# Four of eleven pairs of the first SwiGLU products by seven products of quarters

## The chip, the cores and the metric

The kernel runs on one core of a Trainium2 chip. The metric is the device time of one execution in microseconds (us); it is the median of three runs unless a profiled execution is named. Engines are named as in the profile: PE is TensorE (matmuls) and PEld its weight loads, DVE is VectorE, ACT is ScalarE, POOL is GpSimd, SP is SyncE, which issues most of the loads.

## The reference

Two layers over 512 tokens of width 1024. Each layer is a SwiGLU half step, a token mixer and a second SwiGLU half step, each followed by a layer norm. Four SwiGLUs in all, of hidden width 2816:

```python
def swiglu(x, w13, w2):
    a, b = jnp.split(x @ w13, 2, axis=-1)
    return (jax.nn.silu(a) * b) @ w2

for l in range(DEPTH):
    x = layer_norm(ALPHA * x + 0.5 * swiglu(x, ffn1_w13[l], ffn1_w2[l]), ln_g[l, 0], ln_b[l, 0])
    m = mixer(x, w_in[l], ...)
    x = layer_norm(ALPHA * x + m, ln_g[l, 1], ln_b[l, 1])
    x = layer_norm(ALPHA * x + 0.5 * swiglu(x, ffn2_w13[l], ffn2_w2[l]), ln_g[l, 2], ln_b[l, 2])
```

The change is in `x @ w13`, the first product of a SwiGLU. The mixer is not touched.

## The kernel before

**Arithmetic.** Every float32 operand of a large product is split into a high part (ScalarE copies it to fp32r, line 118) and a low part (VectorE subtracts the high part, line 119). A product is three matmuls: high by high, high by low, low by high. That is `split`, called by `weights` (line 121), which first loads a raw 128 x 1024 block of weights from HBM (line 124, on SP).

**First products.** The hidden width is 22 blocks of 128 features. For block j, `pa` gets the a columns and `pb` the b columns; each is 8 steps of the contraction by 3 matmuls with all 512 tokens as the moving operand (`proj`, line 143). `glu` (line 457) takes silu of `pa` on ScalarE (line 461) and multiplies it with `pb` on VectorE (line 462) into a room `r` of pair k, where k is j modulo 11: block k and block k + 11 make a pair. The pairs go in the order 8, 9, 10, 0 to 7. The first two blocks of a SwiGLU (except the very first) are done by halves of the tokens, 256 columns at a time, because the second half of x comes later.

**Second products.** `Seven` multiplies the activations with w2 by seven products of quarters in place of eight (Strassen's scheme in Winograd's form). It needs sums of quarters on both sides. `activation_sums(k)` (lines 291 to 318) makes those of pair k's activations. `weight_sums(k)` (lines 277 to 289) loads four quarters of w2 into two buffers `ra_w` and `rb_w` (lines 281 and 282, on SP), adds four times on VectorE (lines 283 and 288, three of them in place) and stores each sum to DRAM from POOL's queue (lines 284 and 289). `run` reads the sums back in its own order and does the products. Before the change both sums of pair k come right behind the second block of the pair, so one weight sum goes with every two blocks.

**Buffers.** Tiles of a tag share a fixed number of buffers:

| tag | buffers | what is in it |
|---|---|---|
| raw | 4 | raw weight blocks |
| w | 10 | high and low parts of weights, so five blocks |
| rs | 2 | `ra_w` and `rb_w` of a weight sum; squares of the norm; the changed kernel's rc and rd |
| sa | 3 | silu results, `t1` of a weight sum, `s12` of an activation sum |
| h ("slot") | 33 | x in parts (8), rooms, activation sums, early weights |
| ps | 8 | PSUM banks |

**Order.** The program is written as a straight list. A planner puts each engine's instructions in an order of its own from their dependences and their place in the list, and sets the waits; each engine then runs its list strictly in that order. `flow.tick` only hands out side tasks (transposes of x, the mixer's heads) between matmuls.

The functions that the diff touches:

Of the kernel before, what the change touches and what calls it, by code (L numbers as in the profile page):

```python
# [36 lines left out]
NF = DFF // P  # L40
# [42 lines left out]
def trunk(ctx: ExitStack, tc, x_in, xt_in, w13, w2, w_in, w_br, w_out, ln_g, ln_b, lb_in, hgn, sgg, sgb, sgws,  # L83
          sgbs, masks, tril_in, ident_in, out):
    nc = tc.nc
    V, S, G, PE = nc.vector, nc.scalar, nc.gpsimd, nc.tensor
# [3 lines left out]
    wk = ctx.enter_context(tc.tile_pool(name="wk", bufs=1))  # L90
    psum = ctx.enter_context(tc.tile_pool(name="psum", bufs=8, space=bass.MemoryType.PSUM))

    flow = Flow()
    MM = 216.0

    def bank(name):
        return psum.tile([P, 512], F32, tag="ps", name=name)
# [4 lines left out]
    def slot(name, dtype=F32):  # L102
        return big.tile([P, 2, 512], dtype, tag="h", name=name, bufs=NS)
# [10 lines left out]
    xh, xl = [None] * 4, [None] * 4  # L114


    def split(hi, lo, src):
        S.activation(hi, src, AF.Copy)  # L118
        V.tensor_tensor(lo, src, hi.bitcast(F32), op=ALU.subtract)  # L119

    def weights(src, name, early=False):

        raw = wk.tile([P, D], F32, tag="raw", name=f"r_{name}", bufs=NRAW)
        nc.sync.dma_start(raw, src)
        if early:
            hi, lo = (slot(f"{c}_{name}", F32R).rearrange("p a t -> p (a t)") for c in "hl")
        else:
            hi, lo = (wk.tile([P, D], F32R, tag="w", name=f"{c}_{name}", bufs=NW) for c in "hl")
        split(hi, lo, raw)
        return hi, lo  # L130

    NW = 10
    NS, NRAW, NSA = 33, 4, 3

    def proj(ps, w, c0, mov, nk=KT, n0=0, n=T):

        hi, lo = w
        i = 0
        for k in range(nk):
            cs = slice(c0 + k * P, c0 + (k + 1) * P)  # L140
            mh, ml = mov(k)
            for a, m in ((hi, mh), (hi, ml), (lo, mh)):
                PE.matmul(ps[:, n0:n0 + n], a[:, cs], m[:, n0:n0 + n], start=(i == 0), stop=(i == 3 * nk - 1))  # L143
                i += 1
            flow.tick(3 * MM * n / T)
# [5 lines left out]
    def begin_features():  # L151
        for q in range(4):
            xh[q], xl[q] = slot(f"xh{q}", F32R), slot(f"xl{q}", F32R)
# [26 lines left out]
    H = slice(0, 512), slice(512, 1024)  # L180
# [72 lines left out]
    def quads(name, dtype=F32):  # L253
        return slot(name, dtype).rearrange("p a t -> p (a t)").rearrange("p (q t) -> p q t", q=4)

    NH2 = NF // 2

    class Seven:
# [11 lines left out]

        def part(self, k, a):

            if k not in self.r:
                self.r[k] = quads(f"r{k}")
            return self.r[k][:, a::2, :]

        def weight_sums(self, k):
            w = self.w_of(k)
# [51 lines left out]
        def run(self, c, ln, last):  # L330
# [103 lines left out]
            for tt in range(2):  # L434
# [5 lines left out]
                add_to(xs[t], 0, c, F[tt], sums[t])  # L440
                norm(t, xs[t], sums[t], g, b, last)

    def ffn(l, i, last=False, first_of_all=False):
        made = list(range(Seven.KEPT, NH2)) + list(range(Seven.KEPT))
        seven = Seven(lambda k: w2[l, i, k])
        js = [j for k in made for j in (k, k + NH2)]

        def blocks(j, early=False):
            return (weights(w13[l, i, j], f"a{j}", early), weights(w13[l, i, NF + j], f"b{j}", early),
                    bank(f"pa{j}"), bank(f"pb{j}"))  # L450

        def pair_of(j, args, n0, n):
            wa, wb, pa, pb = args
            proj(pa, wa, 0, from_x, KT, n0, n)
            proj(pb, wb, 0, from_x, KT, n0, n)

        def glu(j, args):
            wa, wb, pa, pb = args
            k, a = j % NH2, j // NH2
            sa = wk.tile([P, T], F32, tag="sa", name="sa", bufs=NSA)  # L460
            S.activation(sa, pa, AF.Silu)
            V.tensor_tensor(seven.part(k, a), sa.rearrange("p (h t) -> p h t", h=2),  # L462
                            pb.rearrange("p (h t) -> p h t", h=2), op=ALU.mult)
            if a:
                seven.activation_sums(k)
                seven.weight_sums(k)

        start = 0 if first_of_all else 2
        first = [blocks(j, True) for j in js[:start]]
        need(0, 1)  # L470
        for z, j in enumerate(js[:start]):
            pair_of(j, first[z], 0, 256)
        need(2, 3)
        for z, j in enumerate(js[:start]):
            pair_of(j, first[z], 256, 256)
            glu(j, first[z])
        for z, j in enumerate(js[start:]):
            if z == 0 and first_of_all:
                begin_features()
                wa = load_wx(w13[l, i, j])  # L480
                for q in range(1, 4):
                    load_xt(q)
                wb = weights(w13[l, i, NF + j], "b0")
                args = wa, wb, bank("pa0"), bank("pb0")
            else:
                args = blocks(j)
            pair_of(j, args, 0, T)
            glu(j, args)
        seven.run(0.5 / ALPHA, (l, 2 * i), last)

    def gates():
# [353 lines left out]
    def load_xt(q):  # L845

        raw = wk.tile([P, D], F32, tag="raw", name=f"xt{q}", bufs=NRAW)
        nc.sync.dma_start(raw, xt_in[q])
        for k in range(2):
            split(xh[q][:, k, :], xl[q][:, k, :], raw[:, k * T:(k + 1) * T])  # L850

    def load_wx(w):

        raw = wk.tile([P, D], F32, tag="raw", name="r_a0", bufs=NRAW)
        hi, lo = (wk.tile([P, D], F32R, tag="w", name=f"{c}_a0", bufs=NW) for c in "hl")
        rx = wk.tile([P, D], F32, tag="raw", name="xt0", bufs=NRAW)
        for z in range(2):
            zs = slice(z * 512, (z + 1) * 512)
            nc.sync.dma_start(raw[:, zs], w[:, zs])
            nc.sync.dma_start(rx[:, zs], xt_in[0, :, zs])  # L860
            split(hi[:, zs], lo[:, zs], raw[:, zs])
            split(xh[0][:, z, :], xl[0][:, z, :], rx[:, zs])
        return hi, lo

    prep = flow.add(prepare(), 30000.0)
    for l in range(DEPTH):
        ffn(l, 0, first_of_all=(l == 0))
        if l == 0:
            flow.finish(prep)
        mixer(l, lb, om)  # L870
        ffn(l, 1, last=(l == DEPTH - 1))
# [98 lines left out]
```

## Time and profile before

| | |
|---|---|
| three runs | 2114.56, 2115.26, 2116.20 us; median 2115.26 |
| profiled execution | 2116.28 us, span 2114.5 us, granted TensorE clock 0.999 |
| busy: PE, DVE, ACT, POOL | 99%, 58%, 36%, 10% of the span |
| DMA | 381 MB, mean 180 GB/s |
| first products of the last SwiGLU | 1758 to 2000 us of the span |
| second product of the last SwiGLU | 2000 to 2098 us |

A line of the profile's groups reads: line, engine, operation, output<-inputs with buffer numbers left out, shape, how often, then busy us and mean ns of one, then the engine's idle time before such instructions and what ended it. A line of the timeline reads: start, length, engine, line, operation, tiles, shape, and in brackets the idle time before it with its releaser. The ends of matmuls are modelled, so spacing is read from starts or from the chain of work that ended last, whose pieces are start, length and what. The DMA lines give count, size and median us from issue to landing.

### The profile page before, as it was taken

How to read it: one execution, taken by the hardware profiler on the slowest of the kernel's cores; microseconds unless marked ns; L12 is line 12 of the kernel's file. 1: busy time of each engine (PE TensorE's matmuls, PEld its weight loads, DVE VectorE, ACT ScalarE, POOL GpSimd, SP SyncE). 2: the span in 40 equal slices, each digit the busy share in tenths (PEclk: the TensorE clock that was granted, in tenths of full speed). 3: DMA queues.
4: the chain of work that ended last, by engine and by line, in shares of the span. 5: the costliest groups of instructions: out<-in, count | busy, mean ns of one | idle time of the engine just before them, and what ended most of it. 6: DMA issues, size and time to landing. Idle time of an engine off the chain costs nothing. (4 is left out here: it accounts for less than half of the span.)

```text
span 2114.5 us, 26531 instructions
## 1 busy us (share of the span) xinstructions
PE 2096.8 (99%) x10024; PEld 1760.8 (83%) x10024; DVE 1226.2 (58%) x2019; ACT 771.4 (36%) x1090; POOL 211.4 (10%) x360
## 2 busy tenths in 40 slices
PE   8999999999999999999999999999999999999998
PEld 6888888888888988888898888888888889888886
DVE  5545578853535745548754456779444456454586
ACT  4222354223422422225522224552343224222363
POOL 0101102001000211101111010020010001110101
PEclk9999999999999999999999999999999999999999
DMA  7665777122242465567756566761222425555674
GB/s 267 216 211 177 247 262 256 44 77 89 81 156 93 176 235 177 195 210 268 248 192 233 178 208 234 270 230 41 90 81 91 143 95 208 205 200 198 223 258 146
DMA packets 113904, 381.01 MB, mean 180 GB/s; under 512 B 14320, under 2 KB 14576, under 8 KB 113776
## 3 DMA queue, kind: packets, MB, share of 16 engines
q1 hardware_dynamic: 88848, 291.68, 42.1%
q0 software_dynamic: 24928, 87.64, 10.9%
q8 instruction: 78, 1.28, 0.3%
q14 instruction: 50, 0.41, 0.1%
HBM read 311.11 MB, written 68.16 MB: 179 GB/s over the span
## 5 line engine op out<-in xcount | busy, mean ns | idle before, releaser
L143 PE MATMUL pa<-xh,h_a 128*128 128x512 f32 (+1 forms) x752 | 284.4, 378 | 6.2 <-ACT xh L118 6.1
L143 PE MATMUL pa<-xl,h_a 128*128 128x512 f32 (+1 forms) x752 | 284.5, 378 | 0.0
L143 PE MATMUL pa<-xh,l_a 128*128 128x512 f32 (+1 forms) x752 | 283.6, 377 | 0.0
L143 PE MATMUL pb<-xh,h_b 128*128 128x512 f32 (+1 forms) x752 | 282.8, 376 | 0.0
L143 PE MATMUL pb<-xh,l_b 128*128 128x512 f32 (+1 forms) x752 | 282.4, 375 | 0.0
L143 PE MATMUL pb<-xl,h_b 128*128 128x512 f32 (+1 forms) x752 | 282.3, 375 | 0.0
L119 DVE TENSOR_TENSOR l_b<-r_b,h_b 128x1024 fp32r<-128x1024 f32 x132 | 161.6, 1225 | 166.8 <-ACT h_b L118 166.3
L118 ACT ACTIVATE h_b<-r_b 128x1024 fp32r<-128x1024 f32 x132 | 140.0, 1061 | 303.6 <-PE pa L143 245.8
L462 DVE TENSOR_TENSOR r<-sa,pb 128x512 f32<-128x512 f32 x88 | 60.6, 688 | 302.0 <-PE pb L143 302.0
L118 ACT ACTIVATE h_a<-r_a 128x1024 fp32r<-128x1024 f32 (+1 forms) x89 | 93.5, 1051 | 274.3 <-PE pb L143 264.7
L143 PEld LDWEIGHTS pa<-xh,h_a 128*128 128x128 f32 x752 | 142.1, 189 | 33.1 <-ACT xh L118 7.4
L143 PEld LDWEIGHTS pa<-xl,h_a 128*128 128x128 f32 x752 | 142.2, 189 | 27.8 <-DVE xl L119 2.0
L143 PEld LDWEIGHTS pa<-xh,l_a 128*128 128x128 f32 x752 | 142.2, 189 | 25.4
L143 PEld LDWEIGHTS pb<-xh,h_b 128*128 128x128 f32 x752 | 141.5, 188 | 25.7
L143 PEld LDWEIGHTS pb<-xl,h_b 128*128 128x128 f32 x752 | 141.5, 188 | 25.6
L143 PEld LDWEIGHTS pb<-xh,l_b 128*128 128x128 f32 x752 | 141.4, 188 | 25.5
L119 DVE TENSOR_TENSOR l_a<-r_a,h_a 128x1024 fp32r<-128x1024 f32 (+1 forms) x89 | 107.8, 1211 | 11.2 <-ACT h_a L118 7.3
L143 PE MATMUL z<-xh,h_z 128*128 128x512 f32 x256 | 102.6, 401 | 0.0
L143 PE MATMUL z<-xh,l_z 128*128 128x512 f32 x256 | 99.8, 390 | 0.0
L143 PE MATMUL z<-xl,h_z 128*128 128x512 f32 x256 | 99.8, 390 | 0.0
L284 POOL DMA_DIRECT2D t<-t x44 | 23.8, 540 | 753.8 <-DVE t L283 687.5
L119 DVE TENSOR_TENSOR l_z<-r_z,h_z 128x1024 fp32r<-128x1024 f32 x32 | 39.2, 1226 | 72.5 <-ACT h_z L118 72.4
(270 smaller groups left out, 4246.3 us busy)
## 6 DMA issues: line engine op xcount, KB each, us to landing
r_b<-in_w_dram SPq DMA_DIRECT2D x88, 512.0 KB, 4.7
r_a<-in_w_dram SPq DMA_DIRECT2D x87, 512.0 KB, 4.8
ra_w<-in_w_dram SPq DMA_DIRECT2D x44, 512.0 KB, 5.4
rb_w<-in_w_dram SPq DMA_DIRECT2D x44, 512.0 KB, 5.0
t<-ra_w POOLq DMA_DIRECT2D x88, 256.0 KB, 2.5
r_c<-in_w_dram SPq DMA_DIRECT2D x44, 512.0 KB, 6.2
r_d<-t SPq DMA_DIRECT2D x44, 512.0 KB, 4.9
r_z<-in_w_in_dram SPq DMA_DIRECT2D x32, 512.0 KB, 3.5
```

The source lines that it names most:

```text
L118: S.activation(hi, src, AF.Copy)
L119: V.tensor_tensor(lo, src, hi.bitcast(F32), op=ALU.subtract)
L143: PE.matmul(ps[:, n0:n0 + n], a[:, cs], m[:, n0:n0 + n], start=(i == 0), stop=(i == 3 * nk - 1))
L284: nc.gpsimd.dma_start(self.t1[k], t1)
L462: V.tensor_tensor(seven.part(k, a), sa.rearrange("p (h t) -> p h t", h=2), pb.rearrange("p (h t) -> p h t", h=2), op=ALU.mult)
```

## The change

In every SwiGLU the pairs 0 to 3 get their first products by seven products of quarters too. The quarters of x are halves of the tokens by halves of the contraction; those of the weights are halves of the contraction by the a and the b columns of a block. `x_sums` makes four sums of x's quarters once in a SwiGLU, with high and low parts. `seven_pair` makes the sums of the weights of the pair's two blocks and does seven products with 256 columns, each with 2 (blocks) x 4 (steps) x 3 matmuls, into four banks, which VectorE and ScalarE combine.

The order changes with it: pairs 8 to 10 as plain blocks, then pairs 0 to 3 by `seven_pair`, then pairs 4 to 7 as plain blocks. Weight sums no longer follow their own pair: four go behind the first four plain blocks (`x_sums` stands ahead of the third), seven behind the first seven plain blocks after the seven pairs. The activation sums of pairs 0 to 3 go behind later plain blocks; the last two stand behind the last block.

```diff
+    def x_sums():
+        lo_t, hi_t = slice(0, 256), slice(256, 512)
+        r = [slot(f"xr{q}") for q in range(4)]
+        for q in range(4):
+            V.tensor_tensor(r[q], xh[q].bitcast(F32), xl[q].bitcast(F32), op=ALU.add)
+        x3 = quads("xs3")
+        for q in range(2):
+            a11, a21, a12, a22 = ...
+            V.tensor_tensor(x3[:, 2 * q:2 * q + 2], a11, a21, op=ALU.subtract)
+            V.tensor_tensor(a21, a21, a22, op=ALU.subtract)
+            V.tensor_tensor(a22, a11, a21, op=ALU.subtract)
+            V.tensor_tensor(a12, a12, a22, op=ALU.subtract)
+            ...
+        for c in ("s2", "s1", "s3", "s4"):
+            hi, lo = (quads(f"x{c}{v}", F32R) for v in "hl")
+            for q in range(2):
+                split(hi[:, 2 * q:2 * q + 2], lo[:, 2 * q:2 * q + 2], parts[c][q])
+    def seven_pair(seven, w13_of, s, k):
+        js = (k, k + NH2)
+        ra = [wk.tile([P, 2, 512], F32, tag="raw", name=f"r_p{j}", bufs=NRAW) for j in js]
+        rc, rd = (wk.tile([P, 2, 512], F32, tag="rs", name=f"r{c}{k}", bufs=2) for c in "cd")
+        t13 = [slot(f"t13{j}") for j in js]
+        t2 = slot(f"t2{k}")
+        for z, j in enumerate(js):
+            wa, wb = w13_of(j), w13_of(NF + j)
+            nc.sync.dma_start(ra[z][:, 0], wa[:, H[0]])
+            nc.sync.dma_start(ra[z][:, 1], wb[:, H[1]])
+            nc.sync.dma_start(rd[:, z], wb[:, H[0]])
+            nc.sync.dma_start(rc[:, z], wa[:, H[1]])
...
+        p = [parts(ra[z], f"p{j}") for z, j in enumerate(js)]
+        for z in range(2):
+            V.tensor_tensor(t13[z], ra[z], rd[:, z:z + 1].broadcast_to([P, 2, 512]), op=ALU.add)
+            V.tensor_tensor(t2[:, z], ra[z][:, 0], t13[z][:, 1], op=ALU.add)
+        w2 = parts(t2, f"t2{k}")
+        wt = [parts(t13[z], f"t{j}") for z, j in enumerate(js)]
+        w21 = parts(rc, f"c{k}", True)
+        V.tensor_tensor(rc, rc, t2, op=ALU.add)
+        w4 = parts(rc, f"d{k}", True)
...
+        A, B, C, E = (bank(f"f{c}{k}") for c in "ABCE")
+        product(A, [p[0][0], p[1][0]], "A11")
+        S.activation(upper, A, AF.Copy)
+        product(B, w2, "s2")
+        V.tensor_tensor(upper, upper, B, op=ALU.subtract)
+        product(C, [wt[0][0], wt[1][0]], "s1")
+        V.tensor_tensor(b1, C, upper, op=ALU.subtract)
+        product(E, [wt[0][1], wt[1][1]], "s3")
+        V.tensor_tensor(b1, b1, E, op=ALU.subtract)
+        product(A, w21, "A12", False)
+        S.activation(lower, A, AF.Silu)
+        product(C, [p[0][1], p[1][1]], "s4", False)
+        V.tensor_tensor(b0, C, upper, op=ALU.subtract)
+        V.tensor_tensor(lower, lower, b0, op=ALU.mult)
+        product(E, w4, "A22", False)
+        V.tensor_tensor(upper, E, upper, op=ALU.add)
+        S.activation(upper, upper, AF.Silu)
+        V.tensor_tensor(upper, upper, b1, op=ALU.mult)
     def ffn(l, i, last=False, first_of_all=False):
...
-            if a:
-                seven.activation_sums(k)
-                seven.weight_sums(k)
...
+                glu(j, first[z])
+                if z == 0:
+                    seven.weight_sums(next(sums))
+        seven.activation_sums(kept)
+        seven.weight_sums(next(sums))
+        for z, j in enumerate(js[2:]):
+            plain(j)
+            if z == 0:
+                s = x_sums()
+            if z < 2:
+                seven.weight_sums(next(sums))
+            if z % 2:
+                seven.activation_sums(kept + (z + 1) // 2)
+        for k in by_seven:
+            seven_pair(seven, w13_of, s, k)
+        rest = by_seven + list(range(S_PAIRS, kept))
+        js = [j for k in range(S_PAIRS, kept) for j in (k, k + NH2)]
+        for z, j in enumerate(js):
+            plain(j)
+            left = len(js) - z - 1
+            if left:
+                seven.weight_sums(next(sums))
+            if left % 2 == 0 or len(rest) > (left + 1) // 2 + 1:
+                seven.activation_sums(rest.pop(0))
+        for k in rest:
+            seven.activation_sums(k)
```

More of the change, by code (lines that the diff above doesn't have):

```diff
@@ L271, in part, with room @@
         def part(self, k, a):
+            return self.room(k)[:, a::2, :]
+        def room(self, k):
             if k not in self.r:
                 self.r[k] = quads(f"r{k}")
-            return self.r[k][:, a::2, :]
+            return self.r[k]
         def weight_sums(self, k):
@@ L441, in run @@
                 norm(t, xs[t], sums[t], g, b, last)
+    def x_sums():
[4 more added lines that the diff above has]
+        x3 = quads("xs3")
+        parts = {"s1": [], "s2": [], "s3": [], "s4": []}
+        for q in range(2):
+            a11, a21, a12, a22 = r[q][:, :, lo_t], r[q][:, :, hi_t], r[q + 2][:, :, lo_t], r[q + 2][:, :, hi_t]
+            V.tensor_tensor(x3[:, 2 * q:2 * q + 2], a11, a21, op=ALU.subtract)
+            V.tensor_tensor(a21, a21, a22, op=ALU.subtract)
+            V.tensor_tensor(a22, a11, a21, op=ALU.subtract)
+            V.tensor_tensor(a12, a12, a22, op=ALU.subtract)
+            for c, v in (("s1", a21), ("s2", a22), ("s3", x3[:, 2 * q:2 * q + 2]), ("s4", a12)):
+                parts[c].append(v)
+        s = {}
+        for c in ("s2", "s1", "s3", "s4"):
+            hi, lo = (quads(f"x{c}{v}", F32R) for v in "hl")
+            for q in range(2):
+                split(hi[:, 2 * q:2 * q + 2], lo[:, 2 * q:2 * q + 2], parts[c][q])
+            s[c] = hi, lo
+        return s
@@ new lines, in seven_pair, with parts, product @@
+    def seven_pair(seven, w13_of, s, k):
[10 more added lines that the diff above has]
+            nc.sync.dma_start(rc[:, z], wa[:, H[1]])
+        def parts(raw, name, early=False):
+            hi, lo = ((slot(f"{v}_{name}", F32R) if early else
+                       wk.tile([P, 2, 512], F32R, tag="w", name=f"{v}_{name}", bufs=NW)) for v in "hl")
+            split(hi, lo, raw)
+            return [(hi[:, z], lo[:, z]) for z in range(2)]
+        p = [parts(ra[z], f"p{j}") for z, j in enumerate(js)]
[7 more added lines that the diff above has]
+        w4 = parts(rc, f"d{k}", True)
+        half = slice(0, 256), slice(256, 512)
+        movs = {"A11": lambda m: (xh[m // 2][:, m % 2, half[0]], xl[m // 2][:, m % 2, half[0]]),
+                "A12": lambda m: (xh[2 + m // 2][:, m % 2, half[0]], xl[2 + m // 2][:, m % 2, half[0]]),
+                "A22": lambda m: (xh[2 + m // 2][:, m % 2, half[1]], xl[2 + m // 2][:, m % 2, half[1]])}
+        for c in s:
+            movs[c] = lambda m, c=c: (s[c][0][:, m], s[c][1][:, m])
+        def product(ps, units, c, first=True):
+            for z in range(2):
+                hi, lo = units[z]
+                for m in range(4):
+                    ms = slice(m * P, (m + 1) * P)
+                    mh, ml = movs[c](m)
+                    for i, (a, v) in enumerate(((hi, mh), (hi, ml), (lo, mh))):
+                        start = first and z == 0 and m == 0 and i == 0
+                        PE.matmul(ps[:, half[z]], a[:, ms], v, start=start, stop=(m == 3 and i == 2),
+                                  skip_group_check=not (first and z == 0))
+                    flow.tick(3 * 120.0)
+        A, B, C, E = (bank(f"f{c}{k}") for c in "ABCE")
+        r = seven.room(k).rearrange("p q t -> p (q t)")
+        lower, upper = r[:, 0:512], r[:, 512:1024]
+        b0, b1 = (wk.tile([P, T], F32, tag="sa", name=f"b{c}", bufs=NSA) for c in "01")
+        product(A, [p[0][0], p[1][0]], "A11")
[15 more added lines that the diff above has]
+        V.tensor_tensor(upper, upper, b1, op=ALU.mult)
@@ L443, in ffn @@
+    S_PAIRS = 4
     def ffn(l, i, last=False, first_of_all=False):
-        made = list(range(Seven.KEPT, NH2)) + list(range(Seven.KEPT))
         seven = Seven(lambda k: w2[l, i, k])
-        js = [j for k in made for j in (k, k + NH2)]
+        w13_of = lambda j: w13[l, i, j]
         def blocks(j, early=False):
-            return (weights(w13[l, i, j], f"a{j}", early), weights(w13[l, i, NF + j], f"b{j}", early),
+            return (weights(w13_of(j), f"a{j}", early), weights(w13_of(NF + j), f"b{j}", early),
@@ L463, in glu @@
                             pb.rearrange("p (h t) -> p h t", h=2), op=ALU.mult)
-            if a:
-                seven.activation_sums(k)
-                seven.weight_sums(k)
[L468 to L486, printed above, removed]
+        kept = Seven.KEPT
+        by_seven = list(range(S_PAIRS))
+        sums = iter(range(NH2))
@@ L487, in ffn, with plain @@
+        def plain(j, args=None):
+            args = args or blocks(j)
             pair_of(j, args, 0, T)
             glu(j, args)
+        js = [j for k in range(kept, NH2) for j in (k, k + NH2)]
+        if first_of_all:
+            begin_features()
+            wa = load_wx(w13_of(js[0]))
+            for q in range(1, 4):
+                load_xt(q)
+            plain(js[0], (wa, weights(w13_of(NF + js[0]), "b0"), bank("pa0"), bank("pb0")))
+            seven.weight_sums(next(sums))
+            plain(js[1])
+        else:
+            first = [blocks(j, True) for j in js[:2]]
+            need(0, 1)
+            for z, j in enumerate(js[:2]):
+                pair_of(j, first[z], 0, 256)
+            need(2, 3)
+            for z, j in enumerate(js[:2]):
+                pair_of(j, first[z], 256, 256)
+                glu(j, first[z])
+                if z == 0:
+                    seven.weight_sums(next(sums))
@@ L489, in ffn @@
+        for z, j in enumerate(js):
+            plain(j)
+            left = len(js) - z - 1
+            if left:
+                seven.weight_sums(next(sums))
+            if left % 2 == 0 or len(rest) > (left + 1) // 2 + 1:
+                seven.activation_sums(rest.pop(0))
+        for k in rest:
+            seven.activation_sums(k)
         seven.run(0.5 / ALPHA, (l, 2 * i), last)
```

## The prediction

> **What bounds the kernel now.** I read the page's first part first, then the waits of TensorE, then the chain of work that ended last, and only then the stretches around the change.
>
> ```profile
> PE 2096.8 (99%) x10024; PEld 1760.8 (83%) x10024; DVE 1226.2 (58%) x2019; ACT 771.4 (36%) x1090; POOL 211.4 (10%) x360
> PE pa L143 <- ACT xh L118: 6.1, 2, 5.7
> PE pE L340 <- DVE l_d L119: 1.6, 2, 1.0
> 1773.57 2.88 PE pb L143 x24
> 1776.44 2.88 PE pa L143 x24
> 1793.11 5.44 PE pa L143 x24
> 1825.75 5.44 PE pa L143 x24
> ```
>
> TensorE is busy 99% of the span and in all of it waits 7.7 us for anybody. So the time is the number of matmuls times their spacing, plus any wait that is newly made. The four lines of the chain (start, length, what) give the spacing in place of the modelled durations: 24 matmuls of 512 columns take 5.44 us, 0.2267 us each; 24 of 256 columns (the first two blocks of a SwiGLU, done by halves of the tokens) take 2.875 us, 0.1198 us each. Half the columns cost 0.528, not 0.500: about 13 ns per matmul do not shrink.
>
> The Trainium skill (TensorE: Matmul & The Clock Gate, Back-to-back issue gap) gives N/2.4 + 2.5 ns, so 215.8 and 109.2 ns; the trace has 226.7 and 119.8 and decides. By the page the gain below would be 2.38 us a pair and 38.0 us in all.
>
> **The matmuls (gain).** A plain pair is 4 x 24 = 96 matmuls of 512 columns: 21.76 us. A pair by seven products is 7 x 2 units x 4 x 3 = 168 matmuls of 256 columns: 168 x 0.1198 = 20.13 us. That is 1.63 us a pair, 6.5 us for the four pairs of a SwiGLU, 26.1 us for the four SwiGLUs (two layers, two each). If nothing is made to wait, 2116.3 (the profiled execution, span 2114.5 and 1.8 around it) becomes 2090.2; the three timed runs have their median 1.0 us lower, 2115.3, so 2089.2 there.
>
> **VectorE and ScalarE in a pair by seven.** Durations by shape, spacing of neighbours from the timeline (all rows here of the last SwiGLU):
>
> ```profile
> L119 DVE TENSOR_TENSOR l_b<-r_b,h_b 128x1024 fp32r<-128x1024 f32 x132 | 161.6, 1225 | 166.8 <-ACT h_b L118 166.3
> L118 ACT ACTIVATE h_b<-r_b 128x1024 fp32r<-128x1024 f32 x132 | 140.0, 1061 | 303.6 <-PE pa L143 245.8 <-PE pb L143 31.2 <-PE pC L340 14.7
> 1848.34 0.43 DVE L307 TENSOR_TENSOR s<-r 128x256 f32<-128x256 f32 x1
> 1848.68 0.69 DVE L283 TENSOR_TENSOR t<-ra_w 128x512 f32<-128x512 f32 x1
> 1849.95 0.69 DVE L288 TENSOR_TENSOR ra_w<-rb_w,ra_w 128x512 f32<-128x512 f32 x1
> 1851.49 0.69 DVE L288 TENSOR_TENSOR ra_w<-ra_w 128x512 f32<-128x512 f32 x1
> 1852.09 1.22 DVE L119 TENSOR_TENSOR l_a<-r_a,h_a 128x1024 fp32r<-128x1024 f32 x1
> 1853.23 0.69 DVE L288 TENSOR_TENSOR rb_w<-rb_w,ra_w 128x512 f32<-128x512 f32 x1
> 1850.00:1900.00 50.00, 50.00 (x223) 41.39 (x222) 26.90 (x40) 14.36 (x19) 6.14 (x12) 1.00 0.57 195
> 2000.00:2050.00 50.00, 50.00 (x222) 41.21 (x221) 43.39 (x59) 31.17 (x43) 5.35 (x10) 1.00 0.78 272
> ```
>
> A 1024-wide operation takes a slot of 1.14 us on VectorE (1852.09 to 1853.23), a 512-wide one 0.60 (1851.49 to 1852.09). A seven pair has seven low parts and three 1024-wide sums, 10 x 1.14, two 512-wide sums and seven combinations, 9 x 0.60: 16.8 us in 20.13, 83%. ScalarE has seven high parts and three evictions, about 9.2 us. The two windows (columns: TensorE, weight load, VectorE, ScalarE, GpSimd busy, clock, DMA) say that such a load is carried: plain blocks keep VectorE at 26.90 of 50 us, but in the second product's stage it is at 43.39, 87%, and TensorE is at 50.00. So inside the pairs I cost VectorE at nothing; what hides it is the other pair's matmuls, four of eight banks being free for it. If that cover fails it is a rival below. Weights of a pair come as eight loads of 256 KB for four of 512: the same bytes, four more issues of 0.33 us on SP, which is idle most of a block. The sums of activations are moved, not added; the last two end behind the last block, in the shade of the second product's first two units, whose operands do not need them. POOL's stores of weight sums are as many as before.
>
> **The sums of x.** Four 1024-wide adds, eight 512-wide differences and eight low parts per SwiGLU: 4 x 1.14 + 16 x 0.60 = 14.2 us of VectorE in one piece, eight half-wide high parts on ScalarE beside it. TensorE has up to two and a half blocks of 10.88 us ahead in the five weight buffers, so by itself it costs nothing. What it does is to stand in front of something: next part.
>
> **The wait that I expect.** The raw right-hand quarters of a seven pair (rc, rd) live in tag "rs", two buffers, the same that every weight sum fills, sums in place, stores and only then frees. Four weight sums go ahead of the first seven pair now, one behind each of the first four blocks, where before there was one in two blocks.
>
> ```profile
> 1783.38 0.69 DVE L283 TENSOR_TENSOR t<-ra_w 128x512 f32<-128x512 f32 x1
> 1784.65 0.68 DVE L288 TENSOR_TENSOR ra_w<-rb_w,ra_w 128x512 f32<-128x512 f32 x1
> 1790.70 0.33 SPq L281 DMA_DIRECT2D ra_w<-in_w_dram  x1
> 1791.60 0.33 SPq L282 DMA_DIRECT2D rb_w<-in_w_dram  x1
> 1793.22 0.69 DVE L462 TENSOR_TENSOR r<-sa,pb 128x512 f32<-128x512 f32 x1 [3.37 <-PE pb L143]
> 1804.10 0.69 DVE L462 TENSOR_TENSOR r<-sa,pb 128x512 f32<-128x512 f32 x1 [3.42 <-PE pb L143]
> 1804.82 0.43 DVE L307 TENSOR_TENSOR s<-r 128x256 f32<-128x256 f32 x1
> 1805.16 0.68 DVE L283 TENSOR_TENSOR t<-ra_w 128x512 f32<-128x512 f32 x1
> 1854.93 0.33 SPq L281 DMA_DIRECT2D ra_w<-in_w_dram  x1
> 1859.77 0.33 SPq L282 DMA_DIRECT2D rb_w<-in_w_dram  x1
> rb_w<-in_w_dram SPq DMA_DIRECT2D x44, 512.0 KB, 5.0
> r_b<-in_w_dram SPq DMA_DIRECT2D x44, 256.0 KB, 4.1
> ```
>
> From a sum's first add to the reload of its second buffer it is 8.2 us undisturbed (1783.38 to 1791.60) and 11.1 when weight splits come between (1848.68 to 1859.77); 5.0 more until the data are there. A cycle is 13 to 16 us, longer than a block. And the order on VectorE looks like program order wherever tiles of a tag are in turn: the weight sum's first add (L283) stands right behind L307, whose tile of tag "sa" is the one before it, though its data had landed by about 1797 (1791.60 + 5.0) and VectorE stood idle for 3.42 us before 1804.10. I take it that buffers of a tag are given out in order of first use. Then the room of the third block (line 462, 1793.22) goes ahead of x_sums' slots, x_sums goes ahead of the third weight sum, and rd comes last.
>
> Worked through on the last SwiGLU, whose blocks lie as before: x_sums from 1793.8 to 1808.0; third weight sum's first add at 1808.0 (its data are there: the second was due at about 1786, + 8.2 + 5.0 = 1799); second buffer reloaded at 1816.2 to 1819.1, landed 1821.2 to 1824.1. The fourth sum's second add waits for that; from there to the first buffer's reuse it is 5.0 us (1849.95 to 1854.93) or 6.1 (1784.65 to 1790.70): 1826.2 to 1830.2. rd lands 4.1 later and its second half 0.3 behind: 1830.6 to 1834.6. Then two times t13 and t2 (3.5), the high part 1.06, the low part 1.22: 5.8, so the second product's weights stand at 1836.4 to 1840.4. TensorE enters the seven pairs at 1825.75 and ends the first product at 1828.6. It is short of work by 7.8 to 11.8 us. About 1 us comes back if the fifth product, whose quarter needs no sum, is put ahead. I take 9.5, nearer the slow end less that 1, since splits of two blocks have piled up behind x_sums. In later pairs nothing like it: rd's buffer is free after t13, and the chain of a pair (load 4.4, sums 3.5, add 1.1, split 2.3, some 12 us) is shorter than 20. In the stage after the pairs seven sums share 87 us; they fall behind by 2 to 4 us a block, but their stores are read only in the second product's units 8 to 10, tens of us later.
>
> **The clock after the wait.** The one long idle time of TensorE in this trace is before its first matmul.
>
> ```profile
> 13.04 0.63 PE L143 MATMUL pa<-xl,h_a 128*128 128x512 f32 x1
> 13.46 0.63 PE L143 MATMUL pa<-xh,l_a 128*128 128x512 f32 x1
> 14.73 0.39 PE L143 MATMUL pa<-xh,h_a 128*128 128x512 f32 x1
> 14.95 0.39 PE L143 MATMUL pa<-xl,h_a 128*128 128x512 f32 x1
> ```
>
> There a matmul takes 0.42 us a step until about 14 and 0.22 after, with the granted clock shown at full. After a 9 us wait the same may return. Bounds: nothing, or the dense slow steps of the start, some 4.5 us at half speed, 2.2 us lost. No row tells, so I take 1.0.
>
> The Trainium skill (TensorE: Matmul & The Clock Gate, What's actually happening) says that an idle window of about 3.4 us halves the clock and about 3.4 us of work restores it. This speaks against the change: 1.7 us a wait, 6.8 us in all in place of my 4.0. The start of the trace agrees with the halving; no row shows it in mid-kernel.
>
> **Sum.** Per SwiGLU -6.5 + 9.5 + 1.0 = +4.0; the first has the same distance of its third block to its seven pairs, so four times: +16. Profiled 2116.3 + 16 = 2132.3, and with the median 1.0 lower 2131. Its own range: wait 6.8 to 11.8 and clock 0 to 2.2 give +0.3 to +7.5 each, 2116 to 2145.
>
> **Rivals.** (a) The change does just what it says, the wait is hidden. For: VectorE carries 87% elsewhere without a wait; if the third weight sum slips ahead of x_sums the chain is up to 9 us shorter (its data are there at 1799) and the wait 0 to 3. Against: the order L307, L283. Between -26.1 and -14: 2089 to 2101. It decides where the wait is under 6.5 us. (b) VectorE becomes the bound in the pairs: it has 3.3 us of slack in 20.1, and each of the combinations frees a bank or feeds the next. At 2 us lost per pair on top of the entry wait, 16 x 2 = 32: 2163. Against: the 43.39 of 50 us window. (c) The wait is about as long as the gain, 6.5 us, by half of x_sums slipping behind: 2111 to 2119.
>
> **How the numbers follow.** Two runs of this kernel differ by up to 0.08%, so 0.2%, 4 us, is about what can be told from no change. Chances: my forecast 0.50 (a tenth of its mass under 2119), (a) 0.30, (c) 0.08, (b) 0.12. So faster 0.30, same 0.13, slower 0.57. The range from 2089 to 2155 leaves out most of (b) and the edge of (a); within the likeliest case it is 2116 to 2145. The predicted time is 2131.
>
> **What would show it.** Right: in each of the four SwiGLUs one idle time of TensorE of 7 to 12 us, about 3 us after the sixth block, ended by the low part of t2; the loads of rd issued several us after the sixth block's middle, released by a store of the fourth weight sum; x_sums in one piece on VectorE ahead of L283; 168 matmuls in 20.1 us in pairs two to four. Wrong: rd loaded before the sixth block ends (then a), idle times between products of later pairs (then b), or 256-wide steps over 0.125 us, since each 0.005 us is 13 us over the 2688 of them.

## The result, and the profile after

The changed kernel takes 2142.39 us (median of four runs, 2141.17 to 2143.84) against 2115.73 for the kernel before: ratio 1.0126, 95% interval 1.0109 to 1.0144. That is 26.7 us slower; 2131 was predicted, with a likeliest range of 2116 to 2145. The profiled execution took 2143.84 us, span 2142.1, mean granted clock 0.987 (before 0.999).

First part of the page and the waits of TensorE (waiting engine and line, what it waits for: us in total, times, longest):

```profile
PE 2081.8 (97%) x11176; PEld 1803.6 (84%) x11176; DVE 1461.6 (68%) x2307; ACT 843.2 (39%) x1186; POOL 212.5 (10%) x360
```

```profile
PE fB L516 <- ACT h_t L119: 42.1, 4, 11.3
PE pa L144 <- ACT xh L119: 6.5, 2, 5.4
PE pa L144 <- DVE xl L120: 0.5, 1, 0.5
```

TensorE is busy 97%, not 99%. The new row is the first of the waits: four times, once in every SwiGLU, the second product of the seven pairs (`fB`) waits for the high part of t2, 42.1 us in all. From start to start of the matmuls around it the four waits are 10.89, 10.11, 11.55 and 10.69 us, 43.2 in all.

The timeline of TensorE around the last of them, and three stretches of it (busy time of TensorE, weight load, VectorE, ScalarE and GpSimd, then granted clock, DMA share, GB/s):

```profile
1849.08 0.28 PE L516 MATMUL fA<-xh,l_p 128*128 128x256 f32 x1
1859.77 0.58 PE L516 MATMUL fB<-xs2h,h_t 128*128 128x256 f32 x1 [10.41 <-ACT h_t L119]
1861.10 0.56 PE L516 MATMUL fB<-xs2h,l_t 128*128 128x256 f32 x1
1864.02 0.41 PE L516 MATMUL fB<-xs2h,h_t 128*128 128x256 f32 x1
1864.23 0.41 PE L516 MATMUL fB<-xs2l,h_t 128*128 128x256 f32 x1
1864.85 0.28 PE L516 MATMUL fB<-xs2l,h_t 128*128 128x256 f32 x1
1864.96 0.28 PE L516 MATMUL fB<-xs2h,l_t 128*128 128x256 f32 x1
```

```profile
1846.40:1859.70 13.30, 2.96 (x25) 2.75 (x23) 8.64 (x12) 2.73 (x4) 1.08 (x2) 0.81 0.79 257
1859.77:1865.00 5.23, 5.07 (x22) 4.71 (x23) 5.23 (x6) 3.27 (x4) 0.00 (x0) 0.52 0.40 131
1871.00:1940.00 69.00, 69.00 (x577) 69.00 (x577) 53.78 (x61) 29.57 (x33) 0.00 (x0) 1.00 0.38 111
```

In the first stretch TensorE does the first product (2.96 us) and then nothing. In the second it works at a granted clock of 0.52: after four longer steps a step is 0.21 us (1864.02 to 1864.23) until 1864.7, then 0.11 to 0.12. In the third, the last three products of pair one and the pairs two to four, it is busy for 69.00 of 69.00 us, with VectorE at 53.78. So the pairs themselves run as planned; the loss is at their entry.

t2 is what the second product multiplies with. It is made of rd, by way of t13 (lines 493 and 494); rc is needed only for the fifth and the seventh product. Why t2 is late is read from the timelines of VectorE and of SyncE's queue, the waits of that queue, and the chain of work that ended last (start, length, what):

```profile
1813.95 0.69 DVE L562 TENSOR_TENSOR r<-sa,pb 128x512 f32<-128x512 f32 x1 [3.08 <-PE pb L144]
1814.56 4.62 DVE L452 TENSOR_TENSOR xr<-xh,xl 128x1024 f32<-128x1024 f32 x4
1828.74 0.68 DVE L287 TENSOR_TENSOR t<-ra_w 128x512 f32<-128x512 f32 x1
1839.81 0.69 DVE L287 TENSOR_TENSOR t<-ra_w 128x512 f32<-128x512 f32 x1 [3.10 <-DMA ra_w<-in_w_dram]
1851.23 1.23 DVE L493 TENSOR_TENSOR t<-r_p,rd 128x1024 f32<-128x1024 f32 x1 [2.69 <-DMA rd<-in_w_dram]
1853.91 1.22 DVE L493 TENSOR_TENSOR t<-r_p,rd 128x1024 f32<-128x1024 f32 x1
1856.80 1.23 DVE L120 TENSOR_TENSOR l_c<-rc,h_c 128x1024 fp32r<-128x1024 f32 x1 [1.67 <-ACT h_c L119]
1857.94 0.68 DVE L494 TENSOR_TENSOR t<-r_p,t 128x512 f32<-128x512 f32 x1
1859.81 1.22 DVE L120 TENSOR_TENSOR l_t<-t,h_t 128x1024 fp32r<-128x1024 f32 x1
```

```profile
1837.64 0.33 SPq L286 DMA_DIRECT2D rb_w<-in_w_dram  x1
1847.91 0.80 SPq L482 DMA_DIRECT2D rd<-in_w_dram  x2
1848.83 0.84 SPq L483 DMA_DIRECT2D rc<-in_w_dram  x2
```

```profile
SPq L482 <- DMA t<-ra_w: 9.3, 1, 9.3
```

```profile
1849.23 6.38 DMA rc<-in_w_dram
1855.71 1.06 ACT h_c L119
1857.94 0.70 DVE t L494
1858.66 2.01 ACT h_t L119 x2
```

`x_sums` lies in one piece from 1814.56 to the third weight sum's first add at 1828.74. The fourth sum begins at 1839.81, 11.1 us later, and rd is issued at 1847.91, after SyncE's queue stood 9.3 us for a store of the fourth sum (`DMA t<-ra_w`). The last lines show something that the prediction did not have: the split of rc stands on VectorE (`l_c`, 1856.80) ahead of the second half of t2 (line 494 at 1857.94). Its inputs had been ready since about 1855.1 (1853.91 + 1.22), so rc cost 2.8 us here.

### The profile page after: what moved, and what is told of

It is laid out like the page before. It is cut to its first block, busy times and chain, and to the rows that moved or that the text cites. A ratio compares the mean times of both kernels' runs of the same rounds, so it can differ in the third digit from the quotient of the medians.

```text
span 2142.1 us, 29271 instructions
## 1 busy us (share of the span) xinstructions
PE 2081.8 (97%) x11176; PEld 1803.6 (84%) x11176; DVE 1461.6 (68%) x2307; ACT 843.2 (39%) x1186; POOL 212.5 (10%) x360
## 4 chain that ended last, share of the span: by engine, by line
PE 44%; issue 3%; DVE 1%; DMA 1%; ACT 1%; POOL 1%; SPq 0%; POOLq 0%; DVEq 0%; ACTq 0%
PE pa L144 5%; PE pb L144 5%; PE z L144 4%; PE pA L344 3%; PE pC L344 3%; PE fC L516 2%; PE fE L516 2%; PE y L226 2%; PE y L144 2%; PE fA L516 2%; PE pB L344 1%; PE pF L344 1%; PE pE L344 1%; PE fB L516 1%; PE q L144 1%
## 5 line engine op out<-in xcount | busy, mean ns | idle before, releaser
L144 PE MATMUL pa<-xh,h_a 128*128 128x512 f32 (+1 forms) x496 | 184.9, 373 | 6.6 <-ACT xh L119 6.5
L144 PE MATMUL pa<-xl,h_a 128*128 128x512 f32 (+1 forms) x496 | 184.9, 373 | 0.5 <-DVE xl L120 0.5
L144 PE MATMUL pa<-xh,l_a 128*128 128x512 f32 (+1 forms) x496 | 184.0, 371 | 0.0
L144 PE MATMUL pb<-xh,h_b 128*128 128x512 f32 (+1 forms) x496 | 183.2, 369 | 0.0
L144 PE MATMUL pb<-xh,l_b 128*128 128x512 f32 (+1 forms) x496 | 182.8, 368 | 0.0
L144 PE MATMUL pb<-xl,h_b 128*128 128x512 f32 (+1 forms) x496 | 182.7, 368 | 0.0
L144 PEld LDWEIGHTS pa<-xl,h_a 128*128 128x128 f32 x496 | 94.2, 190 | 18.2 <-DVE xl L120 2.5
L144 PEld LDWEIGHTS pb<-xl,h_b 128*128 128x128 f32 x496 | 93.5, 189 | 15.7
L144 PEld LDWEIGHTS pb<-xh,h_b 128*128 128x128 f32 x496 | 93.5, 188 | 15.5
L144 PEld LDWEIGHTS pb<-xh,l_b 128*128 128x128 f32 x496 | 93.5, 188 | 15.5
L516 PE MATMUL fB<-xs2h,h_t 128*128 128x256 f32 x128 | 40.2, 314 | 42.1 <-ACT h_t L119 42.1
```

Source lines behind the costliest of these rows:

```text
L516: PE.matmul(ps[:, half[z]], a[:, ms], v, start=start, stop=(m == 3 and i == 2), skip_group_check=not (first and z == 0))
```

## The experiments

Theory: the seven pairs save 26 us; the loss is the late buffer of rd (`x_sums`, then two weight sums, then rd, then rc ahead of t2) and the clock after the wait. Rivals: VectorE can't feed the pairs; the matmuls save less than was worked out; the wait stems from SyncE or from `x_sums` alone. Ratios are to the kernel before, run on the same chip.

**Three weight sums ahead of the pairs**, the other eight behind the eight plain blocks after them.

```diff
-            if z < 2:
+            if z < 1:
                 seven.weight_sums(next(sums))
...
-            if left:
-                seven.weight_sums(next(sums))
+            seven.weight_sums(next(sums))
```

> Three weight sums instead of four ahead of the seven pairs; the fourth goes behind a later plain block. Theory (rd waits for a buffer that the fourth weight sum holds): the two rs buffers are free at about 1834 to 1838 of the last SwiGLU instead of 1848, rd lands some 7 us before the first product ends, the wait of 10 to 11.5 us before the second product goes in all four SwiGLUs and with it the slow clock behind it: 2142.4 - 42.8 - 10 = 2089 to 2092 us. Rival (VectorE is behind at the entry because of x_sums, whatever the buffers do): x_sums is still there, the wait stays within 2 us of 10.7 and the time at 2135 to 2143. Rival (the seven pairs themselves lose time): 2142.

Measured: 2092.53 us, ratio 0.9887 (0.9872 to 0.9902). The chain of the last SwiGLU, first and last product of the pairs:

```profile
1809.64 2.87 PE fA L516 x24
1887.39 2.88 PE fE L516 x24
```

From 1809.64 to 1890.27 it is 80.6 us for 28 products, with no wait between them: four times the 20.13 us of the prediction. One weight sum less ahead of the pairs takes away the wait and the half clock, 50 us. VectorE is thus no bound in the pairs, and the first two rivals fall.

**rc and rd out of the weight sums' buffers**, into slots of tag h.

```diff
-        rc, rd = (wk.tile([P, 2, 512], F32, tag="rs", name=f"r{c}{k}", bufs=2) for c in "cd")
+        rc, rd = (slot(f"r{c}{k}") for c in "cd")
```

> rc and rd in two of the 33 slots (tag h) instead of tag rs, four weight sums ahead as in the change. Theory with order of first use: rd no longer waits for the fourth weight sum's stores, but its slot now comes behind those of the activation sums of pair 10, and these behind the tenth block's silu, which in tag sa stands behind the fourth weight sum's first add. In the trace of the changed kernel the last of them is written at 1844.3 and rd is issued at 1847.9, so 3.5 us are won at most on that path and the wait falls from 10.7 to 6 to 8 us: 2118 to 2130 us. If only the count of rs buffers mattered and not the order of first use, the wait would go: 2090. Rival (rs is not what rd waits for): no change, 2142.

Measured: 2117.66 us, ratio 1.0009 (1.0000 to 1.0019). The waits:

```profile
PE fB L516 <- ACT h_t L119: 10.6, 4, 3.4
PE fB L516 <- DVE l_t L120: 6.4, 4, 1.7
```

The waits fall from 42.1 to 17.0 us, so the buffer is more than half of them. In what stays the order can be seen: SyncE issues rd right behind the fourth sum's reload (1818.48 after 1817.58), VectorE begins t13 only behind the fourth sum's last add (1825.02), and rc's split (1829.56) stands ahead of t2's (1831.36) here too. What each of these costs was not told apart. A buffer taken out of the turn does not take the work out of the queue.

**TensorE kept at work in the gap**: 84 matmuls of 256 columns into a bank that the next product overwrites, between the first and the second product of the first pair (added work that computes nothing).

```diff
+        if k == 0:
+            fh, fl = movs["A11"](0)
+            for i in range(84):
+                PE.matmul(B[:, half[0]], p[0][0][0][:, 0:P], fh, start=True, stop=True, ...)
         product(B, w2, "s2")
```

> 84 extra matmuls of 256 columns (10.1 us) into the bank of the second product, put between the first and the second product of the first seven pair of each SwiGLU: work that is thrown away, the output is that of the reference. The wait itself stays, the idle time of TensorE in it goes. If the slow matmuls after the wait come from the idle time, they go too: the granted clock stays at 1.00 throughout, and the time falls by 4 x 2.5 to 4 x 2.9 us to 2131 to 2133 us, although 336 matmuls were added. Rival (the slow start of the second product is from its operands, not from the clock): no gain, 2142 or a little more.

Measured: 2137.31 us, ratio 1.0100 (1.0085 to 1.0115), granted clock 0.998. The half clock is gone but for the first SwiGLU; yet the time fell by 5.1 us only and misses the expected 2131 to 2133. After its four waits the changed kernel loses 10.5 us in steps longer than 0.12 us (a count over its matmuls). Of these 1.6 stay, behind a gap that the fill left in the first SwiGLU; another 1.6 go to waits at the start of the second SwiGLU that the changed kernel does not have. About 2 come back as waits at the second product: 3.8 us are left there, and only 1.8 of them because the fill (84 x 0.12 = 10.1 us each) is shorter than the wait:

```profile
PE fB L516 <- DVE l_t L120: 2.6, 4, 0.8
PE fB L516 <- ACT h_t L119: 1.2, 1, 1.2
```

The low part of t2 comes some 1.3 us after the high part (1861.03 and 1859.77 in the changed kernel). In the changed kernel this hides in the first long steps, so not all of the 10.5 us is the clock's.

**Two weight sums ahead, nine behind.**

```diff
-            if z < 2:
-                seven.weight_sums(next(sums))
...
-            if left:
+            for _ in range(2 if z == 0 else 1):
                 seven.weight_sums(next(sums))
```

> Only two weight sums ahead of the seven pairs; two behind the first plain block after them, and one behind each other. Theory: as with three, no wait at the entry, 2088 to 2091, with x_sums' place now without any weight sum behind it; nine sums in eight blocks end a little later, hidden in the second product. If three sums leave a short wait this one shows it by being faster. Rival (the sums that were moved behind are missed by the second product): a wait of TensorE appears in the last third of the second product's first stage, and the time is over that of three sums by 4 us or more.

Measured: 2135.76 us, ratio 1.0090 (1.0075 to 1.0105): a miss. The entry wait is gone, and one of the same size stands in the second product. The row of the waits, and the timeline of both queues:

```profile
PE pB L344 <- DVE l_t L120: 36.3, 4, 9.7
```

```profile
2015.23 0.33 SPq L285 DMA_DIRECT2D ra_w<-in_w_dram  x1
2016.45 0.38 SPq L353 DMA_DIRECT2D r_t<-t  x1
2019.39 0.69 DVE L287 TENSOR_TENSOR t<-ra_w 128x512 f32<-128x512 f32 x1 [4.95 <-DMA ra_w<-in_w_dram]
2025.81 1.22 DVE L120 TENSOR_TENSOR l_t<-r_t,h_t 128x1024 fp32r<-128x1024 f32 x1
```

Nine sums don't fit behind eight blocks of 10.88 us: the last one begins at 2019.39, and the second product's weights (`r_t`, then `l_t`) stand behind it in both queues. So, with the buffers as they are, the place for weight sums is bounded on both sides, three or so ahead and eight behind.

**`x_sums` behind the third weight sum**, the four sums ahead kept.

```diff
-            if z == 0:
-                s = x_sums()
             if z < 2:
                 seven.weight_sums(next(sums))
+            if z == 0:
+                s = x_sums()
```

> Four weight sums ahead as in the change, but x_sums behind the third weight sum instead of ahead of it. Theory (x_sums' 14.2 us of VectorE stand ahead of the third weight sum and so push the fourth and rd): the third sum can start when its data land, about 1820 of the last SwiGLU instead of 1828.7; some of that comes back because a store and a reload of 11 us follow; rd is issued some 6 to 9 us earlier and the wait falls from 10.7 to 2 to 5 us: 2096 to 2118 us. Rival (x_sums is not on that path, four cycles of a weight sum alone are too long): the wait stays over 9 us, 2137 to 2143.

Measured: 2121.03 us, ratio 1.0024 (1.0015 to 1.0034). No wait at the entry, but a new one inside the sixth plain block, whose splits now stand behind `x_sums` and the fourth weight sum:

```profile
PE pa L144 <- DVE l_a L120: 9.8, 4, 2.4
PE pb L144 <- ACT h_b L119: 7.4, 4, 3.2
```

This is over the 2096 to 2118 that was expected. From the third block's room to rd's issue it is now 26.6 us (1796.90 to 1823.54), not 34.0 (1813.95 to 1847.91). So `x_sums` does push the weight sums out, as the prediction had it, by 7.3 us at rd. That is less than the wait of 10.7; the rest of it is not seen because TensorE itself comes later, held up in the sixth block. The 14 us of `x_sums` stand in front of the next thing.

**A third buffer in tag rs** (slots cut from 33 to 32 to make room).

```diff
-    NS, NRAW, NSA = 33, 4, 3
+    NS, NRAW, NSA = 32, 4, 3
-        rc, rd = (wk.tile([P, 2, 512], F32, tag="rs", name=f"r{c}{k}", bufs=2) for c in "cd")
+        rc, rd = (wk.tile([P, 2, 512], F32, tag="rs", name=f"r{c}{k}", bufs=3) for c in "cd")
...
```

(The other tiles of tag rs get `bufs=3` in the same way.)

> Tag rs with three buffers (for that 32 slots instead of 33), order as in the change. Theory: rd takes the buffer that the third weight sum frees, at about 1837 instead of 1848, and the fourth sum's first add comes earlier, so the tenth block's silu and the slots of t13 do too; the wait goes or falls under 4 us: 2090 to 2108. Rival (not the buffers but the place in the order): no change, 2142. Rival (33 slots are needed): a new wait in the pairs.

Measured: 2118.38 us, ratio 1.0012 (1.0002 to 1.0021); waits of 4.0 to 5.9 us stay in each SwiGLU, and the time misses the expected 2090 to 2108. rd is early now, and t2 is complete at 1827.1; but rc still comes late, and its split stands ahead of t2's in the queues of both engines:

```profile
1816.14 0.81 SPq L482 DMA_DIRECT2D rd<-in_w_dram  x2
1827.59 0.80 SPq L483 DMA_DIRECT2D rc<-in_w_dram  x2
1831.60 1.06 ACT L119 ACTIVATE h_c<-rc 128x1024 fp32r<-128x1024 f32 x1 [8.97 <-DMA rc<-in_w_dram]
1826.40 0.69 DVE L494 TENSOR_TENSOR t<-r_p,t 128x512 f32<-128x512 f32 x1
1832.69 1.23 DVE L120 TENSOR_TENSOR l_c<-rc,h_c 128x1024 fp32r<-128x1024 f32 x1 [5.59 <-ACT h_c L119]
1834.43 1.22 DVE L120 TENSOR_TENSOR l_t<-t,h_t 128x1024 fp32r<-128x1024 f32 x1
```

**The same, with rc's work behind the second product.** The three lines move down, so that nothing of rc can stand ahead of t2's split.

```diff
-        w21 = parts(rc, f"c{k}", True)
-        V.tensor_tensor(rc, rc, t2, op=ALU.add)
-        w4 = parts(rc, f"d{k}", True)
...
         V.tensor_tensor(upper, upper, B, op=ALU.subtract)
+        w21 = parts(rc, f"c{k}", True)
+        V.tensor_tensor(rc, rc, t2, op=ALU.add)
+        w4 = parts(rc, f"d{k}", True)
         product(C, [wt[0][0], wt[1][0]], "s1")
```

> The third buffer of tag rs stays; in addition the split of rc, its sum with t2 and that sum's split stand behind the second product in the program. Theory (what was left of the entry wait with three buffers is the split of rc standing ahead of t2's split on ScalarE and VectorE): with three buffers t2 was ready at 1827.1, so h_t about 1828.2 and l_t about 1829.4, and the first product ends at 1830.1; the wait before the second product is gone (under 0.5 us in each SwiGLU) and the time falls by 4 x 5.5 and about 1 us of slow clock each, from 2118 to 2090-2096. Rival (the weight sums are still what is late, and rc only stands beside them): 2112-2120, a wait of over 3 us stays.

Measured: 2089.47 us (2089.25 to 2091.5), ratio 0.9877 (0.9862 to 0.9892), the lowest median of all. The waits of TensorE, all that the trace has:

```profile
PE pa L144 <- ACT xh L119: 5.3, 1, 5.3
PE pb L144 <- DVE l_b L120: 0.5, 1, 0.5
PE pE L344 <- DVE l_d L120: 0.3, 2, 0.2
PE pA L344 <- DVE l_c L120: 0.2, 1, 0.2
```

Nothing waits in the pairs, with four weight sums ahead, `x_sums` where the change put it and the same loads on SyncE; so neither `x_sums` nor SyncE alone makes the wait. With the buffer and the place of rc both mended, the whole loss is gone.

**rc's work moved in the changed kernel alone** (the same three lines, two buffers).

> The changed kernel with only the split of rc, its sum with t2 and that sum's split moved behind the second product in the program. Theory: of the 10.7 us wait, 2.9 are rc ahead of t2's split (t2's second add stood behind l_c until 1857.94, and its inputs were there at 1855.1); the rest is rd's late load. So each wait becomes about 7.8 us and the time 2142.4 - 4 x 2.9 = about 2131 (2128-2134). Rival (rd's second half or ScalarE ends the wait in any case): 2140-2144.

Measured: 2132.61 us, ratio 1.0087 (1.0071 to 1.0104), 9.8 us off the changed kernel. The gaps in a SwiGLU, from start to start of the matmuls and summed over its two waits, are 8.55, 7.28, 7.93 and 8.40 us, 8.0 in the mean against 10.8. So rc's part of the wait is 2.8, as in the trace of the changed kernel; rd's late load is left.

```profile
PE fA L513 <- ACT h_c L119: 26.2, 4, 7.2
PE fB L513 <- ACT h_t L119: 3.2, 4, 1.3
```

(Some matmuls of the fifth product went ahead of the second here, hence two rows.)

**rc's work moved with three sums ahead**, a control.

> Three weight sums ahead, and rc's split and sum behind the second product. A control: three sums alone gave 2092.5 with no wait at the entry, so the move has nothing to hide there; theory 2090-2095. If the later place of rc's sums makes the fifth or seventh product of a pair wait (VectorE carries 53.8 of 69 us in the pairs), 16 pairs x 0.5 us or more: over 2100.

Measured: 2092.88 us, ratio 0.9891 (0.9876 to 0.9906), as with three sums alone. The move costs and brings nothing where t2 isn't late.

**More pairs by seven.** Five (three weight sums ahead, one behind each of the first two pairs) and six (one behind each of the first four, an activation sum behind each of the last two), both with rc and rd in slots. The edit for five:

```diff
-        rc, rd = (wk.tile([P, 2, 512], F32, tag="rs", name=f"r{c}{k}", bufs=2) for c in "cd")
+        rc, rd = (slot(f"r{c}{k}") for c in "cd")
...
-    S_PAIRS = 4
+    S_PAIRS = 5
...
             seven_pair(seven, w13_of, s, k)
+            if k < 2:
+                seven.weight_sums(next(sums))
```

> On top of three sums ahead: five pairs by seven products, rc and rd in slots, one weight sum behind each of the first two seven pairs. If TensorE stays the bound: 1.63 us more per SwiGLU, 2092.5 - 6.5 = 2086. VectorE has 141 us of work from the first pair on in 166 us of TensorE (85%, under the 87% that the second product carries). Rival (a weight sum in a pair, 2.4 us, is more than the 3.3 us of slack allow with the order of slots): waits in the first two pairs, 2093 or more.

> The same with six pairs by seven products: a weight sum behind each of the first four, an activation sum behind the last two. If TensorE stays the bound: 2092.5 - 13 = 2079.5. VectorE then has 152 us of work in 164 (93%), and the slots are full (16 for x and its sums, 9 rooms, 9 for a pair, activation sums): I expect waits of 2 to 5 us per SwiGLU, 2085 to 2100.

Measured: five 2100.66 us, ratio 0.9936 (0.9919 to 0.9952), not the 2086 of a TensorE that never waits; six 2114.42, ratio 0.9996 (0.9987 to 1.0005), a miss. With six pairs TensorE waits for VectorE 15 times in the 24 pairs:

```profile
PE fB L516 <- DVE l_t L120: 17.2, 15, 1.9
```

These waits are 1.1 us in the mean. Weight sums share VectorE with the pairs here, and it is busy for 73.48 of 80.00 us (1830 to 1910), 92%. That is the prediction's rival (b), with more pairs than it was stated for. Whether it is VectorE's load or rc's place in the order that makes the low part of t2 late was not told apart at six pairs.

**Five pairs with rc's work moved.**

> Five pairs by seven products, as in the run with five pairs, with rc's split and sum behind the second product. Theory: with five pairs 7-8 us were lost to short waits before the second product, where l_c stood ahead of l_t (1813.53, then 1815.27); these go, and the time is 2086-2094, against 2100.7 without the move. Rival (VectorE is the bound once a weight sum stands between pairs, whatever the order): 2098-2104.

Measured: 2093.71 us, ratio 0.9895 (0.9880 to 0.9909), 7.0 less than without the move. So the order was a part of the loss at five pairs. 4.4 us of waits at the second product stay, of 6.9, and nothing of the fifth pair's 6.5 us is had: four pairs with three sums ahead took 2092.5 and 2092.9. Three buffers together with five pairs were not tried.

## Why the prediction was right

The step at which the forecast turned, the entry wait, came in its place. The stage lies 20.7 us later in the changed kernel's trace (third block's room at 1813.95, not 1793.22). With this shift:

| step | predicted, shifted | measured |
|---|---|---|
| `x_sums` on VectorE | 1814.5 to 1828.7 | 1814.56 to 1828.74 |
| third weight sum's first add | 1828.7 | 1828.74 |
| its second buffer reloaded | 1836.9 to 1839.8 | 1837.64 |
| rd issued | 1846.9 to 1850.9 | 1847.91 |
| first product ends | 1849.3 | 1849.2 |
| t2's low part done | 1857.1 to 1861.1 | 1861.03 (1859.81 + 1.22) |
| TensorE short of work | 7.8 to 11.8 | 10.6 |

- **Matmuls, -26.1 us.** Right. The version without any wait in the pairs is 26.3 us under the kernel before (2115.72 to 2089.47), and a product of 24 matmuls takes 2.88 us in the chains, as predicted.
- **The wait, 9.5 us.** Measured 10.0 to 11.4 us of idle time, 10.7 in the mean (43.2 us less four steps of 0.12, over four). The mechanism holds: `x_sums`, then two weight sums, then rd. Its inside does not quite: the prediction went toward the late end because of splits piled up behind `x_sums`. What was there is rc's split ahead of t2, 2.8 us, which it left out. Without it the wait is 8.0 from start to start, near the early end. So it was partly luck that 9.5 came this near. The 1 us taken off for an early fifth product did not come back either: no matmul of that product stands in the gap.
- **The clock, 1.0 us, with 2.2 as its upper bound.** Mis-sized. The steps after the four waits sum to 3.4, 2.2, 2.3 and 2.6 us over the 0.12 that they take otherwise, 10.5 in all; the bound was taken from the start of the trace and was too low. Keeping TensorE at work took away 8.9 of them, and about 2 came back as waits for t2's low part.
- **The sum.** -26.1 + 42.8 + 10.5 is +27.2 against a measured +26.7; the prediction had -26.1 + 38 + 4 = +16. The 11 us between are 4.8 of wait and 6.5 of clock, less 0.5. Both terms were too small, so no error hid another in the sum.
- **What ends the wait.** The high part of t2, not the low part as named; the low part ends a second, short wait.
- **The weight-sum cycle of 13 to 16 us.** It was counted to the landing of the second buffer, but the next sum's first add needs the first buffer alone: from first add to first add it is 11.1 us here (1828.74 to 1839.81). The nine sums behind the pairs, in the version with two ahead, begin 12.0 us apart in the mean (1923.5 to 2019.39). That is over a block's 10.88, and there it binds.
- **Rivals.** (a), the hidden wait, is what three sums ahead or three buffers with rc behind give, 2089 to 2093, in its forecast range. (b) did not come with four pairs (69.00 of 69.00 us); with six TensorE did wait for VectorE in most pairs. (c) did not come; `x_sums` stayed in one piece.

## What to carry to other kernels

When an edit adds a step whose inputs live in a shared pool of buffers, follow that pool's turn: who holds the buffers, what the holder waits for in its own queue, and which work of the new step stands ahead of the urgent part of it. Here 53 us hung on it (2142.4 against 2089.5), twice what the matmuls saved. Giving the buffer alone, or the order alone, brought 24 and 10 of them; both were needed, unless the work ahead was cut by one weight sum. And when work is pushed away from one stage, count whether it fits in the next: two sums ahead in place of three lost 43 us.

## What the runs showed of the hardware

A wait of TensorE costs more than its length. After each gap of 10.0 to 11.4 us the matmuls took longer steps for 4.0 to 6.7 us, most of them at half pace (granted clock 0.52 in the stretch above), with 2.2 to 3.4 us lost each time. The first four steps, 1.7 us together, are longer than half pace; waits for later splits lie in them, that for t2's low part among them. It does not take so long a gap: in the version with rc and rd in slots, gaps of 1.27 and 1.96 us with about a quarter of a microsecond of work between them were followed by half pace too (1.6 us lost). In the kernel with the fill, single gaps of 1.0 to 1.1 us, and two of 0.92 and 1.05 us in a row, were followed by one longer step. With six pairs one gap of 2.00 us was followed by half pace (1.6 us lost), the other gaps of 1.3 to 2.1 us by one longer step. No length at which it sets in can be given from these runs.

The Trainium skill (TensorE: Matmul & The Clock Gate, What's actually happening) says that the clock is halved after an idle window of about 3.4 us and comes back after about 3.4 us of work, and that the windows run freely. The halving in mid-kernel agrees (steps of 0.21 us against 0.12); the stretches here were 4.0 to 6.7 us, longer than that figure. The estimate of 1.7 us a wait, worked out from it in the prediction, is too little for these gaps by 0.5 to 1.7, the waits in the first steps counted in.
